# Two token blocks of a projection, product by product into two banks

## The chip, the cores and the metric

The kernel runs on one core of a Trainium2 chip. The metric is the time of one execution on the device in microseconds (us), taken as the median of several runs. Before the change it is 278.92 us (three runs: 276.66, 278.92 and 279.52 us).

## The reference

The reference is a decoder trunk of two layers on 256 tokens of 1024 numbers, all in fp32. Each layer has this form (cut):

```python
h = rmsnorm(x, norm_gain[layer])
proj = h @ w_in[j]                     # 1024 x 4104 (layer 0), 1024 x 3328 (layer 1)
qa, ka, va, ga, qb, kb, vb, gb, fb = split_cols(proj, SIZES)
qa, ka, qb, kb = (per-head rmsnorm of each)
ya = attention_a(qa, ka, va);  yb = attention_b(qb, kb, vb)     # layer 1: groups c and d
y = concatenate([ya * silu(ga), yb * silu(gb)], axis=-1)
x = x + y @ w_out[j]
```

Layer 0 has eight heads each of block-sparse and of forgetting attention, layer 1 four heads of differential and eight of sliding-window attention.

## The kernel before

The 256 tokens are two blocks of 128, here block 0 and block 1. The normed input h lies transposed in SBUF in eight tiles of 128 rows (`k` = 0 to 7). To keep fp32 accuracy, every fp32 operand is split into a rounded part and a remainder: h into `hth` and `htl`, each weight tile into `whi` (a CAST on ScalarE, L120) and `wlo` (a subtraction on VectorE, L121). A product of h and w then is three matmuls that add into one PSUM bank: hth x whi (L258), htl x whi (L259), hth x wlo (L260). The piece of h is the stationary operand, the weights are the moving one.

A projection (`proj`) makes up to 512 columns of h @ w for both blocks. Each block adds into a bank of its own, 8 x 3 products deep. The weights come in tiles of two `k` (512 columns) or four `k` (260 or 256 columns). One unit of work takes one weight tile, and does all products of block 0 with it, then all of block 1: six and six for 512 columns, twelve and twelve for the narrower ones. Nine projections run this way: v of group a, q and k (two halves, 260 columns) and v of group b, in layer 1 k and v of group c, q of group d, and k with v of group d (256 columns). Three others are written differently: q and k of group a together (`proj2`, L316, three products to a bank, four banks in turn), q of group c (`t_outer`, all 24 products of block 0, then all of block 1), and the gates and output projections.

After a projection's last unit a generator (`post`) runs in steps, one for each following unit: ScalarE squares each bank, VectorE sums (L343 to L347, in `qk_heads`), later scales (L369), and TensorE transposes the result (L377), from which ScalarE and VectorE write the split operands of the scores (L387 `kf` or `qf`, L394 `khi`, L395 `klo`). For the values, ScalarE copies both banks out (L404).

TensorE's instructions stand in the order in which they are written. The order on ScalarE, VectorE, GpSimd and the DMA queues is made by a scheduler when the program is built, from modelled times of all instructions, and it also gives out the eight banks. Each engine then works strictly in that order. Weight loads go out on SyncE's queue into four raw buffers, and there are five pairs of split tiles (`NW`).

Of the kernel before, what the change touches and what calls it, by code (L numbers as in the profile page):

```python
# [17 lines left out]
KT = D // 128  # L18
# [11 lines left out]
def trunk_kernel(  # L30
# [6 lines left out]
    nc = tc.nc  # L37
# [90 lines left out]
    tiles, wt, units, running = [], [], [], []  # L128
    at = {"unit": 0, "freed": 0}
    H = {}  # L130
# [5 lines left out]
    def unit(need, free, fn):  # L136
        units.append((need, free, fn))
# [119 lines left out]
    def mm3(ps, ah, al, bh, bl, first, last):  # L257
        nc.tensor.matmul(ps, ah, bh, start=first, stop=False)  # L258
        nc.tensor.matmul(ps, al, bh, start=False, stop=False)  # L259
        nc.tensor.matmul(ps, ah, bl, start=False, stop=last)  # L260

    def bank():
        pt = pj.tile([128, 512], F32, name="pj", tag="ps")
        return pt


    def proj(w, c0, n, post, extra=None, sizes=None, t_outer=False, between=None, first=0):
        nn = n + (4 if extra is not None else 0)
        sizes = sizes or ((2, 2, 2, 2) if n > 256 else (4, 4))
        js = [sum(sizes[:i]) for i in range(len(sizes))]  # L270
        base = len(tiles)
        for j, nk in zip(js, sizes):
            parts = [(0, w[j * 128:(j + nk) * 128, c0:c0 + n])]
            if extra is not None:
                parts.append((n, (j, extra)))
            tiles.append((parts, nk, nn))
        ps = []

        def mm(u, t):
            wh, wl = wt[base + u]  # L280
            hth, htl = H["h"]
            c = slice(t * 128, (t + 1) * 128)
            for i in range(sizes[u]):
                k = js[u] + i
                mm3(ps[t][:, 0:nn], hth[:, k, c], htl[:, k, c], wh[:, i, :], wl[:, i, :],
                    k == 0, k == KT - 1)

        if t_outer:
            for t in range(2):
                for half in range(2):  # L290
                    def run(t=t, half=half):
                        if half == 0:
                            ps.append(bank())
                        for u in (2 * half, 2 * half + 1):
                            mm(u, t)
                        if between is not None:
                            between(t, half)
                        if t == 1 and half == 1:
                            running.append(post(ps))
                    unit(base + 2 * half + 2, 2 * t, run)  # L300
            return
        if first:
            ps.extend((bank(), bank()))
        for u in range(first, len(sizes)):
            def run(u=u):
                if u == 0:
                    ps.extend((bank(), bank()))
                for t in range(2):
                    mm(u, t)
                if u == len(sizes) - 1:  # L310
                    running.append(post(ps))
            unit(base + u + 1, 1, run)
        return mm
# [666 lines left out]
```

## Time and profile before

| | us |
|---|---|
| median of three runs | 278.92 |
| lowest and highest run | 276.66, 279.52 |
| the profiled execution's own time | 279.85 |
| its span, first to last instruction | 278.1 |
| TensorE busy in it | 267.6 (96%) |
| VectorE, ScalarE busy | 212.2, 178.6 |

The profiled execution is 0.93 us above the median, and 1.75 us of it lie outside the span. A matmul's shown duration holds its way through the array, which overlaps the next one, so the pace is read from starts, not from durations.

### The profile page before, as it was taken

What the parts mean: (1) busy time and instruction counts of PE and PEld (TensorE: products, weight loads), DVE (VectorE), ACT (ScalarE), POOL (GpSimd) and SP (SyncE); (2) the same over time, 40 slices, a digit from 0 to 9 for tenths busy, and PEclk for the clock granted to TensorE, in tenths of its full rate; (3) what the DMA queues carried; (4) which work ended last, traced back from release to release, by engine and by line L of the source; (5) the groups of instructions that cost most, each with busy time, mean ns of one, the idle gap of its engine ahead of it and who ended that gap; (6) DMA issues with size and microseconds to landing.
All of it is one profiled execution on the core that took longest, in us unless ns stands there. A gap on an engine that the chain in (4) does not pass through costs nothing.

```text
span 278.1 us, 4629 instructions
## 1 busy us (share of the span) xinstructions
PE 267.6 (96%) x1665; PEld 225.7 (81%) x1665; DVE 212.2 (76%) x499; ACT 178.6 (64%) x394; POOL 7.2 (3%) x15
## 2 busy tenths in 40 slices
PE   7999999779999999999999999999999999999994
PEld 2876788558998889999788888888987899897784
DVE  2667998287877549999954988776999888698822
ACT  3469572576687557699742845465785798898500
POOL 6000003000000000000000000000000000000000
PEclk9999999979999999999999999999999999999999
DMA  7974864671444472205855367665508125307012
GB/s 238 202 317 128 225 194 150 195 239 24 148 143 116 118 222 78 77 8 165 247 195 165 90 213 242 212 181 182 167 1 272 35 73 175 132 4 222 5 75 76
DMA packets 26297, 41.38 MB, mean 149 GB/s; under 512 B 1665, under 2 KB 13330, under 8 KB 26274
## 3 DMA queue, kind: packets, MB, share of 16 engines
q1 hardware_dynamic: 26050, 41.04, 47.7%
q0 software_dynamic: 192, 0.04, 1.4%
q8 instruction: 13, 0.21, 0.3%
q14 instruction: 10, 0.08, 0.1%
q10 hardware_dynamic: 32, 0.01, 0.0%
HBM read 40.03 MB, written 1.05 MB: 148 GB/s over the span
## 4 chain that ended last, share of the span: by engine, by line
PE 74%; DMA 9%; DVE 8%; ACT 5%; issue 1%; SPq 1%; ACTq 0%
PE pj L258 21%; PE pj L259 20%; PE pj L260 20%; DMA ytl<-in_w_in_ab_dram 5%; DMA raw<-in_w_in_ab_dram 4%; DVE wlo L121 4%; PE at L509 3%; PE av L551 3%; ACT whi L120 2%; PE at L481 2%; PE at L377 2%; PE at L477 1%; DVE qk_m L344 1%; ACT yb L235 1%; DVE klo L395 1%
## 5 line engine op out<-in xcount | busy, mean ns | idle before, releaser
L121 DVE TENSOR_TENSOR wlo<-raw,whi 128x1024 fp32r<-128x1024 f32 (+1 forms) x70 | 85.2, 1223 | 21.8 <-ACT whi L120 18.3
L120 ACT CAST whi<-raw 128x1024 fp32r<-128x1024 f32 (+1 forms) x70 | 72.4, 1048 | 38.0 <-PE pj L259 20.4
L258 PE MATMUL pj<-whi,hth 128*128 128x512 f32 (+2 forms) x192 | 73.7, 384 | 0.6 <-ACT whi L120 0.5
L260 PE MATMUL pj<-wlo,hth 128*128 128x512 f32 (+2 forms) x192 | 71.2, 371 | 0.5 <-DVE wlo L121 0.5
L259 PE MATMUL pj<-whi,htl 128*128 128x512 f32 (+2 forms) x192 | 71.1, 370 | 0.0
L258 PEld LDWEIGHTS pj<-whi,hth 128*128 128x128 f32 x192 | 36.7, 191 | 8.5 <-ACT whi L120 2.0
L260 PEld LDWEIGHTS pj<-wlo,hth 128*128 128x128 f32 x192 | 36.6, 191 | 8.1 <-DVE wlo L121 1.6
L259 PEld LDWEIGHTS pj<-whi,htl 128*128 128x128 f32 x192 | 36.9, 192 | 5.6
L258 PE MATMUL pj<-hth,whi 128*128 128x256 f32 x128 | 37.0, 289 | 0.0
L260 PE MATMUL pj<-htl,whi 128*128 128x256 f32 x128 | 36.0, 281 | 0.0
L259 PE MATMUL pj<-hth,wlo 128*128 128x256 f32 x128 | 35.9, 281 | 0.0
L258 PE MATMUL pj<-whi,yth 128*128 128x512 f32 (+1 forms) x68 | 26.4, 388 | 0.0
L260 PE MATMUL pj<-wlo,yth 128*128 128x512 f32 (+1 forms) x68 | 25.9, 381 | 0.0
L259 PE MATMUL pj<-whi,ytl 128*128 128x512 f32 (+1 forms) x68 | 25.8, 380 | 0.0
L258 PEld LDWEIGHTS pj<-hth,whi 128*128 128x128 f32 x128 | 24.1, 188 | 0.7 <-issue 0.3
L259 PEld LDWEIGHTS pj<-hth,wlo 128*128 128x128 f32 x128 | 24.2, 189 | 0.0
L260 PEld LDWEIGHTS pj<-htl,whi 128*128 128x128 f32 x128 | 24.1, 188 | 0.0
L490 ACT ACTIVATE e<-e,mn 128x128 f32<-128x128 f32 x32 | 12.5, 390 | 8.9 <-DVE mn L486 8.9
L492 ACT ACTIVATE e<-e,mn 128x256 f32<-128x256 f32 x32 | 15.8, 495 | 0.0
L258 PEld LDWEIGHTS pj<-whi,yth 128*128 128x128 f32 x68 | 12.8, 188 | 2.7 <-issue 0.3
L260 PEld LDWEIGHTS pj<-wlo,yth 128*128 128x128 f32 x68 | 12.8, 188 | 2.6
L259 PEld LDWEIGHTS pj<-whi,ytl 128*128 128x128 f32 x68 | 12.8, 188 | 2.5
(167 smaller groups left out, 390.0 us busy)
## 6 DMA issues: line engine op xcount, KB each, us to landing
raw<-in_w_in_ab_dram SPq DMA_DIRECT2D x28, 512.0 KB, 7.9
raw<-in_w_in_cd_dram SPq DMA_DIRECT2D x26, 512.0 KB, 4.5
raw<-in_w_out_ab_dram SPq DMA_DIRECT2D x8, 512.0 KB, 3.7
raw<-in_w_out_cd_dram SPq DMA_DIRECT2D x8, 512.0 KB, 4.6
xs<-in_x_dram SPq DMA_DIRECT2D x2, 512.0 KB, 6.0
yth<-in_w_in_ab_dram SPq DMA_DIRECT2D x2, 512.0 KB, 7.0
ytl<-in_w_in_ab_dram SPq DMA_DIRECT2D x2, 512.0 KB, 12.7
out_dram<-xs SPq DMA_DIRECT2D x3, 256.0 KB, 2.0
```

The costliest lines, as they stand in the source:

```text
L120: last["act"] = nc.scalar.copy(hi[:, c], raw[:, c])
L121: last["dve"] = nc.vector.tensor_tensor(out=lo[:, c], in0=raw[:, c], in1=hi[:, c].bitcast(F32), op=OP.subtract)
L235: nc.scalar.activation(dump, xs[:, t, :], AF.Square, accum_out=ss[:, t:t + 1])
L258: nc.tensor.matmul(ps, ah, bh, start=first, stop=False)
L259: nc.tensor.matmul(ps, al, bh, start=False, stop=False)
L260: nc.tensor.matmul(ps, ah, bl, start=False, stop=last)
L377: nc.tensor.transpose(pt[:, i, :], qns[t][:, i * 128:(i + 1) * 128], ident)
L481: nc.tensor.matmul(scs[b][:, 128:384], q[r[b], i, :], k[r[b], ik, :], start=n == 0, stop=n == 2)
L490: nc.scalar.activation(e[:, 0:128], e[:, 0:128], AF.Exp, bias=mn[:, 0:1], scale=-1.0, accum_out=sm[:, 0:1])
L492: nc.scalar.activation(e[:, 128:384], e[:, 128:384], AF.Exp, bias=mn[:, 1:2], scale=-1.0, accum_out=sm[:, 1:2])
L509: nc.tensor.transpose(pt[:, i * 128:(i + 1) * 128], blocks[j + i], ident)
L551: nc.tensor.matmul(av[64 * b:64 * b + 64, i, t * 128:256], v[:, t, c:c + 64], p, start=t == 0, stop=t == 1)
```

## The change

In those nine projections, a unit no longer does all products of block 0 and then all of block 1. The loops over `k` and over the three kinds of product are outside, and the loop over the two blocks is the innermost one. The products, their number, their operands and the order within each bank are the same.

```diff
@@ -305,8 +305,14 @@
             def run(u=u):
                 if u == 0:
                     ps.extend((bank(), bank()))
-                for t in range(2):
-                    mm(u, t)
+                wh, wl = wt[base + u]
+                hth, htl = H["h"]
+                for i in range(sizes[u]):
+                    k = js[u] + i
+                    for n, (a, b) in enumerate(((hth, wh), (htl, wh), (hth, wl))):
+                        for t in range(2):
+                            nc.tensor.matmul(ps[t][:, 0:nn], a[:, k, t * 128:(t + 1) * 128], b[:, i, :],
+                                             start=k == 0 and n == 0, stop=k == KT - 1 and n == 2)
                 if u == len(sizes) - 1:
                     running.append(post(ps))
             unit(base + u + 1, 1, run)
```

Lines behind the edit stand six higher in the changed kernel (L343 is L349 there), and all products of these units have line L314.

First place, TensorE, the first tile of the first changed projection (v of group a; `pj_422` is the bank of block 0, `pj_423` that of block 1). Before, the first eight rows:

```order
L258 MATMUL pj_422<-whi_363,hth_105 128x512
L259 MATMUL pj_422<-whi_363,htl_106 128x512
L260 MATMUL pj_422<-wlo_364,hth_105 128x512
L258 MATMUL pj_422<-whi_363,hth_105 128x512
L259 MATMUL pj_422<-whi_363,htl_106 128x512
L260 MATMUL pj_422<-wlo_364,hth_105 128x512
L258 MATMUL pj_423<-whi_363,hth_105 128x512
L259 MATMUL pj_423<-whi_363,htl_106 128x512
```

Now:

```order
L314 MATMUL pj_422<-whi_363,hth_105 128x512
L314 MATMUL pj_423<-whi_363,hth_105 128x512
L314 MATMUL pj_422<-whi_363,htl_106 128x512
L314 MATMUL pj_423<-whi_363,htl_106 128x512
L314 MATMUL pj_422<-wlo_364,hth_105 128x512
L314 MATMUL pj_423<-wlo_364,hth_105 128x512
L314 MATMUL pj_422<-whi_363,hth_105 128x512
L314 MATMUL pj_423<-whi_363,hth_105 128x512
```

The bank changes at every product instead of every sixth, `wlo` is first read by the fifth product instead of the third, and both banks are complete only at the end of the last unit.

Second place, ScalarE, behind the last unit of that projection (`v` the copies of its two banks, `qf`, `qhi`, `kf` the operands of the first scores of group a, the CASTs the splits of later weight tiles). Before:

```order
L120 CAST whi_575<-raw_573 128x1024
L404 ACTIVATE v_522<-pj_422,n_r_325 128x512
L120 CAST whi_633<-raw_630 128x1040
L404 ACTIVATE v_522<-pj_423,n_r_325 128x512
L387 ACTIVATE qf_109<-at_525,pcol_90 128x512
L394 ACTIVATE qhi_110<-at_531,pcol_90 128x512
L120 CAST whi_652<-raw_649 128x1040
L387 ACTIVATE kf_112<-at_558,pcol_90 128x512
```

Now:

```order
L120 CAST whi_575<-raw_573 128x1024
L410 ACTIVATE v_522<-pj_422,n_r_325 128x512
L410 ACTIVATE v_522<-pj_423,n_r_325 128x512
L393 ACTIVATE qf_109<-at_525,pcol_90 128x512
L400 ACTIVATE qhi_110<-at_531,pcol_90 128x512
L120 CAST whi_633<-raw_630 128x1040
L120 CAST whi_652<-raw_649 128x1040
L393 ACTIVATE kf_112<-at_558,pcol_90 128x512
```

The second copy, `qf` and `qhi` now stand ahead of the CAST of `whi_633`; `kf` stays behind that of `whi_652`.

Third place, VectorE, behind the last unit of q of group d in layer 1 (`sq_2099`, `sq_2103` the squares of its two banks; `klo` the remainder operand of group c's scores, which TensorE reads soon after). Before:

```order
L121 TENSOR_TENSOR wlo_2199<-raw_2196,whi_2198 128x1024
L344 TENSOR_REDUCE qk_m8_2098<-sq_2099 128x8
L347 TENSOR_SCALAR qk_m8_2098<-qk_m8_2098,n_em_1870 128x8
L121 TENSOR_TENSOR wlo_2247<-raw_2244,whi_2246 128x1024
L344 TENSOR_REDUCE qk_m8_2098<-sq_2103 128x8
L395 SCALAR_TENSOR_TENSOR klo_1785<-at_2107,pcol_90,khi_1784 128x4x128
L347 TENSOR_SCALAR qk_m8_2098<-qk_m8_2098,n_em_1870 128x8
L395 SCALAR_TENSOR_TENSOR klo_1785<-at_2115,pcol_90,khi_1784 128x4x128
```

Now:

```order
L121 TENSOR_TENSOR wlo_2199<-raw_2196,whi_2198 128x1024
L121 TENSOR_TENSOR wlo_2247<-raw_2244,whi_2246 128x1024
L350 TENSOR_REDUCE qk_m8_2098<-sq_2099 128x8
L350 TENSOR_REDUCE qk_m8_2098<-sq_2103 128x8
L353 TENSOR_SCALAR qk_m8_2098<-qk_m8_2098,n_em_1870 128x8 x2
L401 SCALAR_TENSOR_TENSOR klo_1785<-at_2107,pcol_90,khi_1784 128x4x128
L401 SCALAR_TENSOR_TENSOR klo_1785<-at_2115,pcol_90,khi_1784 128x4x128
```

The first reduction, which stood ahead of the subtraction `wlo_2247`, now stands behind it, so both reductions are between it and `klo`. On ScalarE the CAST of `whi_2246` moves ahead of both squares in the same way.

## Rows read from the trace of the kernel before

**Rows 1.** The page: TensorE's busy time, its granted clock by slice, the chain.

```profile
PE 267.6 (96%) x1665; PEld 225.7 (81%) x1665; DVE 212.2 (76%) x499; ACT 178.6 (64%) x394; POOL 7.2 (3%) x15
...
PEclk9999999979999999999999999999999999999999
...
PE 74%; DMA 9%; DVE 8%; ACT 5%; issue 1%; SPq 1%; ACTq 0%
```

**Rows 2.** Groups by line and shape, TensorE: count, then busy us and mean ns.

```profile
L258 PE MATMUL pj<-whi,hth 128*128 128x512 f32 x144 | 59.7, 415 | 0.6 <-ACT whi L120 0.5
...
L258 PE MATMUL pj<-whi,hth 128*128 128x260 f32 x32 | 9.3, 292 | 0.0
...
L258 PE MATMUL pj<-whi,hth 128*128 128x256 f32 x16 | 4.7, 293 | 0.0
```

**Rows 3.** Timeline of TensorE, `t_outer`: first and last of 24 products into one bank.

```profile
163.19 0.40 PE L258 MATMUL pj<-whi,hth 128*128 128x512 f32 x1
...
168.50 0.40 PE L260 MATMUL pj<-wlo,hth 128*128 128x512 f32 x1
```

**Rows 4.** The same, `proj2`: first and last of 22 products, bank changed every third.

```profile
29.34 0.39 PE L260 MATMUL pj<-wlo,hth 128*128 128x512 f32 x1
...
34.19 0.40 PE L260 MATMUL pj<-wlo,hth 128*128 128x512 f32 x1
```

**Rows 5.** The same, v of group a: 46 products, bank changed every sixth.

```profile
35.25 0.39 PE L260 MATMUL pj<-wlo,hth 128*128 128x512 f32 x1
...
45.68 0.40 PE L260 MATMUL pj<-wlo,hth 128*128 128x512 f32 x1
```

**Rows 6.** Timeline of ScalarE, 44 to 57 us.

```profile
45.17 0.68 ACT L404 ACTIVATE v<-pj,n_r 128x512 f32<-128x512 f32 x1
50.53 1.06 ACT L120 CAST whi<-raw 128x1040 fp32r<-128x1040 f32 x1 [4.67 <-DMA raw<-in_w_in_ab_dram]
51.50 0.68 ACT L404 ACTIVATE v<-pj,n_r 128x512 f32<-128x512 f32 x1
...
54.73 1.06 ACT L120 CAST whi<-raw 128x1040 fp32r<-128x1040 f32 x1 [1.39 <-DMA raw<-in_w_in_ab_dram]
55.69 0.68 ACT L387 ACTIVATE kf<-at,pcol 128x512 f32<-128x512 f32 x1
```

**Rows 7.** Timeline of TensorE, 52 to 62 us.

```profile
52.23 0.66 PE L377 MATMUL at<-ident,e 128*128 128x128 f32 x4 [2.07 <-ACT v L404]
...
56.43 0.49 PE L477 MATMUL at<-kf,qf 64*128 64x128 f32 x4 [0.75 <-ACT kf L387]
...
60.82 0.63 PE L260 MATMUL pj<-wlo,hth 128*128 128x512 f32 x1
61.25 0.63 PE L258 MATMUL pj<-whi,hth 128*128 128x512 f32 x1
```

**Rows 8.** Windows: stretch, length, busy times by engine, granted clock, DMA share, GB/s.

```profile
55.30:58.70 3.40, 1.62 (x14) 0.85 (x14) 2.76 (x4) 3.18 (x5) 0.00 (x0) 1.00 0.71 229
58.80:62.10 3.30, 3.30 (x18) 2.59 (x14) 3.18 (x17) 2.10 (x10) 0.00 (x0) 0.50 0.78 245
62.20:66.50 4.30, 4.30 (x20) 3.50 (x19) 2.57 (x4) 3.08 (x9) 0.00 (x0) 1.00 0.14 49
```

**Rows 9.** Timeline of ScalarE, 190 to 196 us.

```profile
192.25 1.05 ACT L120 CAST whi<-raw 128x1024 fp32r<-128x1024 f32 x1 [0.56 <-PE pj L259]
193.21 0.59 ACT L343 ACTIVATE sq<-pj 128x512 f32<-128x512 f32 x1
```

**Rows 10.** Timeline of VectorE, 190 to 197 us.

```profile
193.34 1.23 DVE L121 TENSOR_TENSOR wlo<-raw,whi 128x1024 fp32r<-128x1024 f32 x1 [0.65 <-PE at L377]
194.48 0.68 DVE L344 TENSOR_REDUCE qk_m<-sq 128x8 f32<-128x512 f32 x1
195.07 0.74 DVE L395 SCALAR_TENSOR_TENSOR klo<-at,pcol,khi 128x512 fp32r<-128x512 f32 x1
195.73 0.22 DVE L347 TENSOR_SCALAR qk_m<-qk_m,n_em 128x8 f32<-128x8 f32 x1
195.86 0.75 DVE L395 SCALAR_TENSOR_TENSOR klo<-at,pcol,khi 128x512 fp32r<-128x512 f32 x1
```

**Rows 11.** Timeline of TensorE, 190 to 197.7 us: the first product with `klo`.

```profile
196.66 0.39 PE L481 MATMUL at<-klo,qhi 64*128 64x256 f32 x2
```

## Prediction

> **What bounds the kernel now.** I read the page first: TensorE is busy 96% of the span and holds 74% of the chain, nearly all of it the split products, and its clock is at the upper level nearly throughout [rows 1]. So the pace of products decides, and next the few places where TensorE stands still. The groups by shape give the number of products in the edited loop [rows 2]. The 144 products of 512 columns at L258 stand for 432 with L259 and L260; the code takes 96 of these for `proj2` and 48 for `t_outer`, which leaves 288 in six edited projections. With 32 x 3 = 96 of 260 columns and 16 x 3 = 48 of 256, 432 products are reordered.
>
> **Pace.** The timeline shows three stretches at full clock that differ in how often the bank changes. Inside one bank 23 intervals take 168.50 - 163.19 = 5.31 us, 230.9 ns each [rows 3]. With a change at every third product 21 intervals, seven of them changes, take 4.85 us, 231.0 ns each [rows 4]. In the first projection that is edited, a change at every sixth, 45 intervals, seven of them changes, take 10.43 us, 231.8 ns [rows 5]. If a change saved x, rows 4 would be x/3 shorter than rows 3. They agree within 0.1 ns, so with starts given to 0.01 us x is 0 within some 2 ns either way, or 288 x 2 = 0.6 us over the kernel. I take 0. The stationary operand changes at every product before and after, and which operand is shared by neighbours leaves no mark either, since L259 (shared weights) and L260 (other weights) stand in these stretches alike.
>
> The Trainium skill ("TensorE: Matmul & The Clock Gate", section "Back-to-back issue gap") gives columns / 2.4 plus 2.5 ns, 216 ns for 512 columns, and no term for the bank. The measured 231 ns is longer, so the row decides. By the page at most 15 ns of a product could be won, an estimated 288 x 15 = 4.3 us; by the rows nothing.
>
> **The first `wlo` read comes two products later.** That is 0.46 us of grace per unit. No wait for `wlo` stands in front of an edited unit in the stretches read, so it is worth 0.
>
> **The bank of block 0 is complete later.** It ended six (or twelve narrow) products before the unit did, 6 x 231 = 1.39 us; now it ends one before, 1.16 us later. The scheduler answers with another order on ScalarE and VectorE. SyncE's and GpSimd's orders are unchanged, so the weight loads only move if their buffers do. Transposes follow a step or more later, several units of 12 x 231 = 2.77 us, which covers the delay at seven of the nine ends. The other two are these.
>
> *Place one, 45 to 57 us.* TensorE lost 2.07 us at 52.23, because the second copy `v`, which frees the bank, was queued behind a CAST that waited 4.67 us for its load [rows 6, 7]. In the new order this copy, `qf` and `qhi` come ahead of that CAST, so this stall goes. What is late next: `kf` is still behind the second CAST, which waited for its own load until 54.73. It ran at 55.69, and the scores waited for it until 56.43. Loads keep their issue order and land no earlier. TensorE then reaches the scores about 2.3 us earlier and waits until 56.43 all the same. The 2.07 us are moved, not won: 0. The bounds are -2.07 us (if the second load lands early enough) and 0.
>
> *Place two, 192 to 197 us.* The first product with `klo` starts at 196.66 [rows 11], and the second `klo` ends at 195.86 + 0.75 = 196.61 [rows 10]. There is no slack, so its delay is TensorE's. In the new order:
> - The CAST waited for the last reader of `whi` [rows 9], which is now one product earlier: 192.25 - 0.23 = 192.02.
> - The subtraction starts 1.09 us after it, as before (193.34 - 192.25), at 193.11, and the next instruction 1.14 us later (194.48 - 193.34): first reduction 194.25.
> - The second reduction follows 0.59 us later (195.07 - 194.48), at 194.84, and ends after 0.68 us at 195.52. The two short scalings take until about 195.65.
> - Two `klo` follow, 0.66 us apart, the last ending at 195.65 + 0.66 + 0.75 = 197.06, 0.45 us later than before. The squares they need start 0.96 us after the CAST (193.21 - 192.25), at 192.98, and are not late.
>
> Price +0.45 us; bounds 0 (if the scalings fit the gaps) and +0.7 us (if the CAST comes no earlier). Everything behind it moves along, since TensorE leads the rest.
>
> **Clock.** After the standstills at 52 to 58 us the granted clock fell to half, 1.2 GHz, from 58.8 to 62.1 us; before and behind it is at 2.4 GHz [rows 8]. Products then start 0.43 us apart [rows 7], so these 3.3 us cost 3.3 x (0.43 - 0.231) / 0.43 = 1.5 us. In the new order the standstill is one piece of about 3.2 us ahead of 56.43. The half clock may come a little earlier, where TensorE waits anyway, or stay once. I take no change, with bounds -1.5 us (no such stretch) and +1.5 us (twice).
>
> **Sum.** 0 + 0 + 0 + 0.45 + 0 = +0.45 us. Against the profiled execution that is 279.85 + 0.45 = 280.3 us; that execution is 0.93 us above the median, and against the median it is 278.92 + 0.45 = **279.4 us**.
>
> **Rivals.**
> 1. *Adding into the bank of the neighbour costs something that a single change does not show.* For it: at half clock a product takes 0.43 us, so at full clock it could take 0.215 us, 16 ns less than the 231 seen [rows 7]; something limits only the full clock. If alternation removed this, 288 x 16 = 4.6 us and about 144 x 8 = 1.2 us for the narrow ones (half the columns) are won: 279.4 - 5.8 = 273.6 us. Against it: rows 3 to 5, where even one change in three should show 5 ns. Chance 6%.
> 2. *A moved evacuation lands behind a CAST that itself waits for the unit under way* (slower). Most CASTs late in the kernel wait for TensorE [rows 9], and the new order puts several in front of squares and copies. Where what follows has no slack, TensorE waits up to one unit: 2.77 us, 279.4 + 2.8 = 282.2 us. It decides once the delay is over the slack, as at `klo`. Against it: only that one place had a slack near zero; elsewhere the transposes come units later. Chance 7%.
> 3. *The clock oscillates.* If changing banks at every product opened small gaps in which the clock falls, and each of the nine projections lost one such stretch as priced above, it is 9 x 1.5 = 13.5 us: 293 us. Two stretches decide. Against it: rows 4 change banks every 0.7 us and the clock in their slices stays up [rows 1]. Chance 3%. The Trainium skill (same page, section "A second HAM failure mode: psum-queue depth-cycling") reports this for a 512-column kernel that cycles through banks; by that rule this change is a loss, and the trace does not bear it out.
> 4. *Place one pays after all*, alone or with the lost half-clock stretch: 279.4 - 2.1 - 1.5 = 275.8 us. Chance 3%.
>
> That the products would not alternate is excluded by the built order.
>
> **Numbers.** The forecast, little change, has 81%. About 1%, 2.8 us, is what a measurement of this kernel tells from no change. Faster is rival 1 with 6% and 2 of the 3% of rival 4 (over 2.8 us only with both its parts), 8%; slower is rivals 2 and 3, 10%; within 1% are the remaining 82%. The range takes the clock's bounds around 279.4: 279.4 - 1.5 - 0.45 = 277.4, and 279.4 + 1.5 + 0.25 = 281.2. The runs of before scatter down to 276.66, so I put the lower end at 276.8 and the upper at 281.3.
>
> **What would show it.** Starts 231 ns apart in the edited units (about 215 would be rival 1). No wait of L377 for `v` near 50 us, but 3 us at the first scores for `kf`. A wait of about 0.45 us for `klo` at the first scores of group c. One half-clock stretch near 56 to 62 us. The prediction is wrong if the pace differs by over 5 ns, or if TensorE stands over 1 us anywhere behind 62 us.

## The result and the profile after

| | before | changed |
|---|---|---|
| median of 20 runs each, us | 277.87 | 279.78 |
| lowest and highest run, us | 276.66, 281.04 | 278.42, 281.06 |
| ratio, 95% interval | | 1.0063, 1.0042 to 1.0084 |
| profiled execution: own time, span, us | 279.85, 278.1 | 279.90, 278.1 |

The change costs 0.63%, +1.75 us (+1.2 to +2.3). (The ratio is an estimate over the fast runs, not the quotient of the two medians, which is 1.0069.) That is inside "within 1%" and inside the range, but four times the +0.45 us of the forecast. The two profiled executions are equally long, so their difference can't show where the 1.75 us are; the experiments had to.

The page after, which answers to [rows 1]:

```profile
PE 266.9 (96%) x1665; PEld 225.0 (81%) x1665; DVE 211.9 (76%) x499; ACT 178.7 (64%) x394; POOL 7.2 (3%) x15
...
PEclk9999999959999999999999999999999999999999
...
PE 84%; DVE 5%; DMA 5%; ACT 4%; SPq 1%; issue 0%
```

Busy times are the same. In the clock line the ninth slice shows 5 where it showed 7. The timeline of TensorE, v of group a, first and last row of 23 that hold two products each (x2: one product into each bank):

```profile
35.10 0.63 PE L314 MATMUL pj<-whi,htl 128*128 128x512 f32 x2
...
45.32 0.63 PE L314 MATMUL pj<-wlo,hth 128*128 128x512 f32 x2
```

44 intervals take 10.22 us, 232.3 ns each, against 231.8 ns in [rows 5]. Over the whole kernel the median interval of 512 columns is 232 ns in both, and that of 260 and 256 columns 120 and 118 ns in both. The pace has not moved.

Place one, the timeline of ScalarE (in brackets: idle time before, and what ended it):

```profile
45.75 1.27 ACT L410 ACTIVATE v<-pj,n_r 128x512 f32<-128x512 f32 x2 [0.54 <-PE pj L314]
...
49.55 1.06 ACT L120 CAST whi<-raw 128x1040 fp32r<-128x1040 f32 x1 [1.37 <-DMA raw<-in_w_in_ab_dram]
53.26 1.06 ACT L120 CAST whi<-raw 128x1040 fp32r<-128x1040 f32 x1 [2.65 <-PE pj L314]
54.22 0.68 ACT L393 ACTIVATE kf<-at,pcol 128x512 f32<-128x512 f32 x1
```

The timeline of TensorE there:

```profile
52.63 0.62 PE L314 MATMUL pj<-wlo,hth 128*128 128x512 f32 x2
54.95 0.49 PE L483 MATMUL at<-kf,qf 64*128 64x128 f32 x4 [1.70 <-ACT kf L393]
56.11 0.39 PE L487 MATMUL at<-khi,qhi 64*128 64x256 f32 x2 [0.67 <-ACT khi L400]
...
60.43 1.05 PE L314 MATMUL pj<-wlo,hth 128*128 128x512 f32 x2
61.28 1.05 PE L314 MATMUL pj<-whi,hth 128*128 128x512 f32 x2
```

The copies `v` run at 45.75, and the wait for `v` of [rows 7] is gone. The scores wait for `kf` instead, 1.70 us, because `kf` is behind the second CAST, and that CAST waited for its load. (Its bracket names TensorE, whose last product ended at the same time; but the last part of the load landed at 53.16, and in e1, e4 and e5 below the bracket of the same CAST names the load.) The loads of this execution landed earlier than those of [rows 6]: the two CASTs that waited until 50.53 and 54.73 run at 49.55 and 53.26. The windows (length, busy times, granted clock, DMA share, GB/s), which answer to [rows 8]:

```profile
53.00:54.90 1.90, 0.26 (x2) 0.00 (x0) 0.56 (x1) 1.65 (x3) 0.00 (x0) 1.00 0.79 281
55.00:56.50 1.50, 0.83 (x8) 0.55 (x8) 1.50 (x3) 1.06 (x2) 0.00 (x0) 1.00 0.79 285
56.60:63.30 6.70, 6.34 (x25) 5.13 (x24) 3.85 (x19) 4.71 (x18) 0.00 (x0) 0.50 0.63 192
```

TensorE stands still for 1.70 us, is busy for 0.83 of the next 1.50 us, on the scores, and then the clock is at 1.2 GHz from 56.54 to 63.37, 6.83 us, where before it was 3.41 us (58.75 to 62.16).

Place two, the timeline of VectorE, which answers to [rows 10]:

```profile
193.02 1.23 DVE L121 TENSOR_TENSOR wlo<-raw,whi 128x1024 fp32r<-128x1024 f32 x1 [1.56 <-ACT whi L120]
194.16 1.27 DVE L350 TENSOR_REDUCE qk_m<-sq 128x8 f32<-128x512 f32 x2
195.35 0.35 DVE L353 TENSOR_SCALAR qk_m<-qk_m,n_em 128x8 f32<-128x8 f32 x2
195.61 1.40 DVE L401 SCALAR_TENSOR_TENSOR klo<-at,pcol,khi 128x512 fp32r<-128x512 f32 x2
```

That of TensorE, which answers to [rows 11]:

```profile
196.44 0.28 PE L487 MATMUL at<-khi,qlo 64*128 64x256 f32 x2
197.07 0.39 PE L487 MATMUL at<-klo,qhi 64*128 64x256 f32 x2 [0.35 <-DVE klo L401]
```

Before, the last of these two followed 0.12 us behind the one ahead of it; now 0.63 us. The step costs 0.51 us where it happens (0.35 us of it are the idle time in the bracket).

TensorE's products and transposes are numbered from 0 at the beginning of the program. The starts of the same number show how the executions drift apart. (Inside an edited unit the same number is another product of that unit. Executions differ by some tenths before any change acts; e2, e9 and e10 are experiments told below.)

| product | start before, us | changed - before | e2 - before | e10 - e9 |
|---|---|---|---|---|
| 150 | 40.36 | -0.16 | +0.02 | +0.39 |
| 205 | 53.43 | -2.41 | -0.83 | -1.04 |
| 219 | 57.59 | -1.48 | -0.54 | -1.08 |
| 245 | 63.53 | -0.13 | -2.07 | -0.13 |
| 360 | 77.80 | -0.16 | -2.11 | +1.27 |
| 1100 | 195.89 | -0.11 | -2.05 | +1.27 |
| 1110 | 196.67 | +0.41 | -1.54 | +1.78 |
| 1165 | 205.14 | +0.39 | -1.56 | +1.78 |
| 1260 | 218.92 | +0.03 | -1.92 | +1.43 |
| 1664 | 274.14 | +0.02 | -1.92 | +1.43 |

Column three reads: the changed kernel is 2.41 us ahead when the wait for `v` is gone, still 1.48 us ahead at the scores (its loads came early), and has lost that lead behind the longer half-clock stretch. The 0.5 us at 196 us come, and 0.39 us of them are given back at 206 and 219 us. The last of these in TensorE's timeline, before:

```profile
218.22 0.49 PE L477 MATMUL at<-kf,qf 64*128 64x128 f32 x4
218.91 0.39 PE L481 MATMUL at<-khi,qhi 64*128 64x256 f32 x2 [0.21 <-ACT khi L394]
```

The same with the change:

```profile
218.47 0.49 PE L483 MATMUL at<-kf,qf 64*128 64x128 f32 x4
218.95 0.39 PE L487 MATMUL at<-khi,qhi 64*128 64x256 f32 x2
```

TensorE comes 0.25 us later and finds `khi` at the same time: a wait that was there before takes up half of the delay.

### The profile page after: what moved, and what is told of

It reads as the page before. It is cut to its first block, busy times and chain, and to the rows that moved or that the text cites. A ratio compares the mean times of both kernels' runs of the same rounds, so it can differ in the third digit from the quotient of the medians.

```text
span 278.1 us, 4628 instructions
## 1 busy us (share of the span) xinstructions
PE 266.9 (96%) x1665; PEld 225.0 (81%) x1665; DVE 211.9 (76%) x499; ACT 178.7 (64%) x394; POOL 7.2 (3%) x15
## 3 DMA queue, kind: packets, MB, share of 16 engines
HBM read 40.03 MB, written 1.05 MB: 148 GB/s over the span
## 4 chain that ended last, share of the span: by engine, by line
PE 84%; DVE 5%; DMA 5%; ACT 4%; SPq 1%; issue 0%
PE pj L314 29%; PE pj L258 14%; PE pj L260 13%; PE pj L259 13%; DMA ytl<-in_w_in_ab_dram 5%; PE at L515 3%; PE av L557 3%; DVE wlo L121 2%; PE at L487 2%; PE at L383 2%; ACT whi L120 2%; DVE klo L401 1%; PE at L483 1%; ACT e L498 1%; PE at L198 1%; ACT e L496 1%
## 5 line engine op out<-in xcount | busy, mean ns | idle before, releaser
L314 PE MATMUL pj<-whi,hth 128*128 128x512 f32 (+2 forms) x144 | 42.1, 374 | 0.0
L314 PE MATMUL pj<-whi,htl 128*128 128x512 f32 (+2 forms) x144 | 40.5, 363 | 0.0
L314 PE MATMUL pj<-wlo,hth 128*128 128x512 f32 (+2 forms) x144 | 40.3, 361 | 0.0
L314 PEld LDWEIGHTS pj<-wlo,hth 128*128 128x128 f32 x144 | 26.0, 192 | 4.4
L314 PEld LDWEIGHTS pj<-whi,htl 128*128 128x128 f32 x144 | 26.0, 192 | 4.4
L314 PEld LDWEIGHTS pj<-whi,hth 128*128 128x128 f32 x144 | 24.9, 192 | 4.4 <-issue 0.6
L258 PE MATMUL pj<-whi,hth 128*128 128x512 f32 x48 | 19.6, 408 | 2.3 <-ACT whi L120 2.3
L260 PE MATMUL pj<-wlo,hth 128*128 128x512 f32 x48 | 19.2, 401 | 0.5 <-DVE wlo L121 0.5
L259 PE MATMUL pj<-whi,htl 128*128 128x512 f32 x48 | 19.0, 395 | 0.0
```

Of the source, the lines that this page charges most:

```text
L314: nc.tensor.matmul(ps[t][:, 0:nn], a[:, k, t * 128:(t + 1) * 128], b[:, i, :], start=k == 0 and n == 0, stop=k == KT - 1 and n == 2)
```

## The experiments

**The theory** after the result: the loss is the clock. Removing the wait for `v` joins two short standstills into one ahead of the first scores, and more executions then have a longer half-clock stretch. **The rivals**: the alternation itself costs something in all nine projections; or the loss sits at the `klo` step and others like it. They were timed in three sets (e1 to e4, e5 to e8, e9 to e12), each on another chip, 12 or 13 runs of each kernel next to 35 of the kernel before.

One view goes through all of them. The mean granted clock of an execution tells how long the clock was down: in the profiled ones 0.998 and more goes with no half-clock stretch in the body of the kernel, 0.992 to 0.994 with one of 3.41 us, 0.987 and 0.988 with one of 6.83 us. All executions fall into three groups around these values (0.997 and more, 0.991 to 0.994, 0.986 to 0.988), with nothing between. The group tells how long the clock was down; where, only the profiled executions show. Number of executions, and their median time in us:

| kernel | none | 3.4 us | 6.8 us |
|---|---|---|---|
| before (three sets of 35) | 52: 277.2 to 277.6 | 49: 278.9 to 279.1 | 4: 280.4 to 280.6 |
| e2, all but v of group a | 7: 277.68 | 5: 279.11 | 0 |
| e3, q of group d alone | 6: 277.62 | 6: 279.18 | 0 |
| changed | 0 | 8: 278.92 | 12: 280.12 |
| e1, v of group a alone | 0 | 4: 278.98 | 8: 280.28 |
| e4, all but q of group d | 0 | 5: 278.63 | 7: 279.79 |
| e5, changed, with filler products | 12: 277.60 | 1: 279.89 | 0 |

Leaving out e5's single run, the kernels agree down a column within 0.6 us (0.8 in the last), and along a row it is 1.2 to 1.7 us from one column to the next. What differs between the kernels is which columns they fall into.

### One projection at a time: e1 to e4

All four give `proj` a flag that chooses between the old and the new loop. e1 sets it for v of group a alone, e2 for all others, e3 for q of group d alone (the projection behind place two), e4 for all others:

```diff
-    def proj(w, c0, n, post, ..., first=0):
+    def proj(w, c0, n, post, ..., first=0, alt=False):
...
+                if alt:
...
+                else:
+                    for t in range(2):
+                        mm(u, t)
...
-    proj(w_ab, 1024, 512, lambda ps: values(ps, "va", 0, 512))
+    proj(w_ab, 1024, 512, lambda ps: values(ps, "va", 0, 512), alt=True)
```

e1, expected:

> Alternates only the projection v of group a; every other projection as before. ScalarE's order at its end is that of the change (both copies ahead of the waiting CAST), the order at klo is that of before. Theory clock (the standstill at the scores of group a is one piece now, so the half-clock stretch behind it is 6.8 us instead of 3.4 us in most executions): about +1.2 us, ratio 1.004, a half-clock stretch of about 6.8 us near 56 to 63 us, no wait for klo at 196 us. Theory order at klo (the whole loss is the wait for klo and other late evacuations): ratio 1.000. Theory pace (alternating products are slower by a fixed amount, 288 wide ones cost the 1.9 us): 48 of 288, +0.3 us, 1.001.

Measured: 280.11 us, ratio 1.0066 (1.0037 to 1.0094). In the list of TensorE's waits (us in total, times, longest):

```profile
PE at L487 <- ACT kf L397: 2.1, 1, 2.1
```

The window behind it, in which the clock is at half:

```profile
57.20:63.90 6.70, 6.39 (x26) 5.03 (x24) 4.59 (x20) 4.42 (x17) 0.00 (x0) 0.50 0.61 186
```

The whole loss is there with one projection of nine. In the traces, ScalarE's and VectorE's orders in e1 differ from those of the kernel before only between 45 and 55 us, by what the change moves there.

e2, expected:

> Alternates all projections but v of group a. ScalarE's order at 45 to 56 us is that of before, the one at klo that of the change. Theory clock: the half-clock stretch is as before (3.4 us), and only the wait for klo is left: +0.5 us, ratio 1.002. Theory order at klo: the full loss, 1.006. Theory pace: 240 of 288 wide products, +1.6 us, 1.0055.

Measured: 277.87 us, ratio 1.0002 (0.9972 to 1.0031). The waits at place one:

```profile
PE at L387 <- ACT v L414: 1.2, 1, 1.2
...
PE at L487 <- ACT kf L397: 1.0, 1, 1.0
```

The windows there and behind it:

```profile
50.00:57.00 7.00, 4.12 (x22) 2.87 (x20) 3.71 (x4) 5.32 (x8) 0.00 (x0) 1.00 0.70 225
57.00:64.00 7.00, 6.59 (x39) 5.31 (x40) 4.69 (x21) 5.13 (x18) 0.00 (x0) 1.00 0.64 196
```

240 of the 288 wide products and all narrow ones alternate, and no loss shows, though the interval reaches up to 0.3%. Inside the classes e2 is 0.46 and 0.18 us above the kernel before of its set (277.22 and 278.93 us); e3, below, which alternates q of group d alone, is 0.40 and 0.25 us above. So the alternation as such has no price beyond what place two costs. In the traces, ScalarE's and VectorE's orders in e2 differ from those of the changed kernel only around place one. TensorE stands there for about as long in sum as in e1, in two pieces with products between them, and in this execution the clock stays up. The table of starts shows what that is worth: against the kernel before, whose execution had 3.41 us of half clock, e2 goes from 0.54 to 2.07 us ahead between the products 219 and 245.

e3, expected:

> Alternates only q of group d. Both theories of order expect the wait of about 0.5 us for klo at 196 us; theory clock: +0.5 us in all, ratio 1.002, with the clock of before; theory order at klo: most of the 1.9 us, 1.005; theory pace: +0.3 us for 48 of 288 products, 1.001.

Measured: 278.47 us, ratio 1.0011 (0.9986 to 1.0037). The step at `klo` is 0.49 us, read from starts as above, and the executions fall into the classes as before. The profiled one has waits of 1.08 us for `v` and 0.92 us for `kf`, and still a stretch of 3.41 us (58.40 to 61.81): two pieces make a stretch rarer and shorter, they do not exclude it.

e4, expected:

> Alternates all projections but q of group d: no wait for klo (under 0.1 us at 196 us). Theory clock: the standstill ahead of the scores and the long half-clock stretch stay, +1.2 us, ratio 1.004. Theory order at klo: 1.000 to 1.001. Theory pace: +1.6 us, 1.0055.

Measured: 279.35 us, ratio 1.0038 (1.0014 to 1.0062); no wait over 0.2 us for `klo` at place two, 1.9 us for `kf` at place one. In each class e4 is 0.3 us below the changed kernel, which was timed in another set. That, the 0.25 to 0.40 us of e3 and the traces (0.1 us left at the end in the changed kernel, 0.3 us in e3) put place two at 0.1 to 0.4 us; most of the loss stays without it.

### Filler products: e5

The changed kernel, and TensorE does 14 more products where it would stand. Their results are overwritten by the scores.

```diff
+        hx = H["h"][0]
+        if grp == "a" and i == 0:
+            for _ in range(8):
+                nc.tensor.matmul(scs[0], hx[:, 0, 0:128], hx[:, 0:2, :], start=True, stop=True)
...
+        if grp == "a" and i == 0:
+            for _ in range(6):
+                nc.tensor.matmul(scs[0][:, 128:384], hx[:, 0, 0:128], hx[:, 0, :], start=True, stop=True)
```

Expected:

> The changed kernel with 8 wide and 6 narrow products of h with itself put in front of the first scores of group a, into the bank that the scores then overwrite: they fill the standstill and compute nothing that is used. Theory clock: the granted clock does not fall near 56 to 63 us (mean granted clock 0.997 or more in most executions, against 0.988 and 0.993), and the loss goes: about 277.7 us, ratio 0.999 to 1.001, although TensorE does more. Theory order or pace: the loss stays or grows by the added products, ratio 1.006 to 1.010.

Measured: 277.62 us, ratio 0.9973 (0.9947 to 1.0000). TensorE's timeline at the first scores:

```profile
53.21 1.99 PE L485 MATMUL at<-hth 128*128 128x512 f32 x8
56.84 0.49 PE L487 MATMUL at<-kf,qf 64*128 64x128 f32 x4 [1.65 <-ACT kf L393]
57.26 1.42 PE L491 MATMUL at<-hth 128*128 128x256 f32 x6
```

More work, `kf` no earlier, and the loss is gone: 12 of 13 executions have no half-clock stretch. (The profiled one is the thirteenth; its second CAST waited for its load until 55.15, and even behind the filler the scores waited 1.65 us for `kf`.) In the class without a stretch, 277.60 us stands against 277.57 of the kernel before in the same set. The order of ScalarE and VectorE is that of the changed kernel but for a few instructions near 69 us. The filler takes nothing off the way of `kf`, and the scores still come behind it; what it takes away is the stretch. This is what shows the clock to be the cause, and not the wait itself.

### Moving the first scores: e6 to e12

The call below starts the two halves of group a's scores at given units. If the scores came later, `kf` would be ready and the wait gone. e6, e7 and e8 move them to units 3 and 6, in the kernel before, in the changed one, and in e4's:

```diff
-    play(12, {1: [heads_a(0)], 5: [heads_a(1)]})
+    play(12, {3: [heads_a(0)], 6: [heads_a(1)]})
```

Expected:

> The kernel before, with the two halves of the scores of group a started two units and one unit later (3 and 6 instead of 1 and 5), so that TensorE has products to do while kf is on its way. Theory clock: no wait for kf, no half clock, the wait for v near 50 us (1 to 2 us) stays; the 2.1 us of waits at the scores and the mean 0.6 us of half clock are won: about 275.2 us, ratio 0.990. Rival: the waits only move to a later place (loads of the next weight tiles), 0.998 to 1.002.

> The changed kernel with the same later start of the scores. Theory clock and place one: without the standstill the earlier copy of v pays, the wait for v near 50 us is gone, only the 0.5 us at klo is lost: 1 us under the shifted kernel before, about 274.2 us, ratio 0.987, so that the change is worth -0.4% here where it cost +0.6%. Theory order or pace: still 1.7 us slower than the shifted kernel before, ratio 0.996.

> As the shifted changed kernel, but q of group d as before the change, so without the wait for klo: 0.5 us less, about 273.7 us, ratio 0.985; a version that beats both kernels. Rival: the klo wait is hidden behind something else, no difference.

Measured: ratios 0.9969 (0.9940 to 0.9998), 1.0048 (1.0021 to 1.0075) and 1.0012 (0.9982 to 1.0043). All three missed. In e6 new waits of 1.0 us (for `mn`) and 0.6 us stand at 71 to 74 us, in e8 one of 3.3 us at 70 us. By classes e6 has 10, 1 and 1 executions, e7 0, 7 and 5, e8 1, 8 and 3. In e7 the waits of place one are gone, and in the list of TensorE's waits a larger one is new:

```profile
PE at L515 <- DVE mn L494: 4.1, 1, 4.1
```

TensorE stands from 70.8 to 74.9 us, and the clock is down from 74.39 to 77.81. The halves are three units apart instead of four: the second half's scores now stand right ahead of the first half's transposes, and these start only when VectorE has read the first of those scores (L494, at 74.34). That they wait for the bank of these scores is likely, but not shown. The wait moved, and the clock with it. So the distance was kept next: units 2 and 6 in e9 (the kernel before), e10 (the changed one) and e11 (e4's), units 3 and 7 in e12 (e4's).

> The kernel before, with the scores of both halves of group a one unit later (2 and 6 instead of 1 and 5), so that their distance of four units stays and the waits seen near 70 to 75 us in the two earlier shifted kernels do not come. Theory clock: the waits at the scores (2.1 us) go, the wait for v near 50 us stays, full clock: about 275.2 us, ratio 0.990.

> The changed kernel, shifted in the same way. Theory clock: no standstill at all near 45 to 60 us, only the 0.5 us at klo lost: 1 us under the shifted kernel before, about 274.2 us, ratio 0.986. Theory order or pace: 1.7 us over the shifted kernel before.

> As the changed kernel shifted by one unit, with q of group d as before the change: 0.5 us less, about 273.7 us, ratio 0.984. A version meant to beat both kernels.

> The same with the scores two units later (3 and 7): as e11_shift26_no_qd within 0.5 us if one unit already covers the way of kf and khi; lower if a wait for them is left there.

| | us | ratio, interval | none / 3.4 us / 6.8 us |
|---|---|---|---|
| e9, before | 275.99 | 0.9915, 0.9883 to 0.9947 | 11 / 1 / 0 |
| e10, changed | 277.39 | 0.9971, 0.9945 to 0.9998 | 12 / 0 / 0 |
| e11, e4's | 277.69 | 0.9953, 0.9924 to 0.9983 | 10 / 2 / 0 |
| e12, e4's, 3 and 7 | 278.27 | 0.9989, 0.9962 to 1.0015 | 1 / 11 / 0 |

e9 beats both kernels. In the class without a stretch it takes 275.94 us against 277.31 of the kernel before, so the wait for `kf` is gone too. e10 missed: with the clock up in all its runs, it was expected under e9 and is 1.45 us over it in the class without a stretch, near the 1.7 us that its expectation gave to order or pace. The last column of the table of starts places this: 1.4 us are lost around 67 to 74 us, at the projections of q and k of group b. The timeline of VectorE in e9:

```profile
67.48 0.22 DVE L615 SCALAR_TENSOR_TENSOR z<-pj,n_r,bfor 128x4 f32<-128x4 f32 x1
...
67.69 1.22 DVE L121 TENSOR_TENSOR wlo<-raw,whi 128x1024 fp32r<-128x1024 f32 x1
68.83 0.22 DVE L615 SCALAR_TENSOR_TENSOR z<-pj,n_r,bfor 128x4 f32<-128x4 f32 x1
...
70.97 0.68 DVE L369 TENSOR_TENSOR qn<-pj,rs_r2x 128x512 f32<-128x512 f32 x1
```

The same stretch in e10:

```profile
67.69 1.22 DVE L121 TENSOR_TENSOR wlo<-raw,whi 128x1024 fp32r<-128x1024 f32 x1
...
68.92 1.21 DVE L121 TENSOR_TENSOR wlo<-raw,whi 128x1024 fp32r<-128x1024 f32 x1
70.05 0.34 DVE L621 SCALAR_TENSOR_TENSOR z<-pj,n_r,bfor 128x4 f32<-128x4 f32 x2
...
72.45 1.27 DVE L375 TENSOR_TENSOR qn<-pj,rs_r2x 128x512 f32<-128x512 f32 x2
```

TensorE's timeline in e10, behind it:

```profile
67.84 1.39 PE L515 MATMUL at<-ident,e 128*128 128x128 f32 x11 [0.43 <-DVE rs_t2x L177]
...
73.18 0.97 PE L483 MATMUL at<-kf,qf 64*128 64x128 f32 x3 [0.31 <-DVE qn L375]
```

With both banks complete only at the end of the unit, `z` can't slip in between the subtractions, and `qn`, which frees a bank for the next scores, comes 1.48 us later. This is the second rival of the prediction, real but in another kernel: in the order of units that the change met it cost nothing, as column three of the table of starts is flat from 63 to 195 us. e11 and e12 missed too; their profiled executions show waits of the same kind (2.3 us for `rs_t2x` at 67 us in e11, 2.3 us for `mn` at 76 us in e12), and in each the clock fell within 0.3 us of the end of that wait.

## Why the prediction was right, and the term that was mis-sized

The measured time is inside the range, but the sum is not why. The term that the sum prices, place two, brought 0.1 to 0.4 us, and most of the loss came from the clock, which it puts at 0. That 279.78 us lies so near the forecast 279.4 us is luck: the median of three runs that the sum starts from, 278.92 us, is 1.05 us above that of twenty.

- **Pace: right.** 232.3 ns against 231.8. Rival 1 is out, and so is rival 3: in e2, where 384 of 432 products alternate, 7 of 12 executions have no half-clock stretch, and none has the long one. The section "A second HAM failure mode: psum-queue depth-cycling" of the page "TensorE: Matmul & The Clock Gate" in the Trainium skill tells of a kernel that cycles through banks, idles briefly between groups of products, and has an oscillating clock. Here the alternation opened no such gap (232.3 ns from start to start), and the clock did not oscillate. Where it fell in the middle of the kernel, TensorE was standing still or had just done so. The prediction's "at most 15 ns" by the section "Back-to-back issue gap" of the same page was no bound: the Trainium skill calls that figure the gap of an isolated product.
- **`wlo`, 0: right.** No edited unit has a wait for it over 0.1 us, before or after.
- **Place one, moved and not won: right in kind.** The wait for `v` went and the one for `kf` came, 1.7 to 2.1 us in the profiled executions of the changed kernel, e1 and e4, not the 3 us forecast. That "loads land no earlier" holds for the order of loads, not for an execution: the second CAST, behind its load, starts at 53.26 in the changed kernel and at 55.15 in e5, whose orders up to there are the same, and the length of this wait goes with it.
- **Place two, +0.45: right where it happens** (0.51 us), but the sentence "everything behind it moves along" failed: existing waits at 206 and 219 us took up 0.39 us of it, and little more than 0.1 us reached the end of this execution.
- **Rival 4, place one pays:** out. It would have left less of the half clock; there is more.
- **Clock, 0 with a bound of +1.5 us for "twice": the mis-sized term.** The prediction saw that the standstill becomes one piece and priced a second stretch rightly, and then chose "once" from one profiled execution, as if the length of the stretch belonged to the kernel. It is a matter of chances, and the change shifts them: from 52, 49 and 4 of 105 executions with none, one and two lengths to 0, 8 and 12 of 20. With the medians of before, about 277.4, 279.0 and 280.5 us, the old counts give a mean of 278.3 us and the new ones 279.9 us: the classes alone make +1.6 us. The changed kernel's own medians, 278.92 and 280.12 us, are 0.1 and 0.4 us lower, from another set, so that inside a class nothing more is lost. That it is the clock is shown by e5, that it is this one place by e1 and e2.

The profiled execution of before was one with a stretch, 0.93 us above the median. That could have raised the suspicion that other executions had none, and that "none" was what stood to be lost.

What stays open: why one execution of a program has a stretch and the next none, or the long one. The landing times of the loads differ too, but no run set them apart from the clock. The profiled executions of e2 and e3 have nearly the same waits at place one (1.2 and 1.0 us, 1.1 and 0.9 us), the one without a stretch and the other with one.

## What to carry to other kernels

Where a granted clock falls behind a standstill, ask how many executions it falls in, not whether; a step that joins two short standstills into one can lose more in the clock (1.6 us here) than it wins in waits (2.8 us in the profiled execution before, 1.7 to 2.1 us with the change in e1, e4 and the changed kernel). Before removing a wait, look what the engine reaches next, and when it is ready: TensorE was better off in e2 and e3, waiting twice for some 1 us with products between, than in e1 and e4, waiting once for some 2 us. And a small delay is only worth what no later wait takes up, so follow the starts of the same instruction in both traces to the end of the span.

## What the runs showed of the hardware

- The bank that a product adds into is free of charge: a change at every product, every third, every sixth or never gives 231 to 232 ns for 512 columns.
- Half-clock stretches in the middle of the kernel were 3.4 or 6.8 us long in every profiled execution that had one, and the time came in steps to match, some 1.2 to 1.7 us each.
- Fourteen useless products, about 2.6 us of work in an idle place (8 x 0.23 and 6 x 0.12), made the changed kernel 0.9% faster (0.9973 against 1.0063, measured in different sets against the same kernel).
